# S5 mixer and ConvFFN layer: the SSM's output products with channels in partitions, and the GLU's operands split in place

## The chip, the cores and the metric

The kernel runs on one core of a Trainium2 chip. The metric is the device time of one execution in microseconds (us); lower is better. Engines are named as in the profile: PE is TensorE (PEld its weight loads), DVE is VectorE, ACT is ScalarE, POOL is GpSimd, SP is SyncE, which here only issues transfers.

## The reference, cut to what matters

One layer on a sequence of 2048 frames of 1024 channels with 16 meta tokens ahead of it: an S5 state-space mixer with a GLU, then a gated ConvFFN, both with a pre-RMSNorm and a residual.

```python
def s5_mixer(xn, w_in, lam_re, lam_im, log_dt, b_re, b_im, c_re, c_im, d_skip, w_glu):
    u = (xn @ w_in).reshape(bsz, L, S5_GROUPS, S5_GROUP)      # 64 groups of 16 channels
    ...                                                       # discretised a, b per group, 64 complex states
    _, _, s_re, s_im = lax.associative_scan(_complex_lin_combine, (a_re, a_im, bu_re, bu_im), axis=1)
    y = (einsum('ghp,blgp->blgh', c_re, s_re) - einsum('ghp,blgp->blgh', c_im, s_im) + d_skip * u)
    y = jax.nn.gelu(y.reshape(bsz, L, D_MODEL))
    a, g = jnp.split(y @ w_glu, 2, axis=-1)
    return a * jax.nn.sigmoid(g)

h = concatenate([meta, x])
h = h + s5_mixer(rms_norm(h, norm_mix), ...)
h = h + conv_ffn(rms_norm(h, norm_ffn), ...)                   # up, causal conv of 3, silu gate, down
return h[:, N_META:]
```

## The kernel before

**The sequence in chunks.** The 2048 frames are 128 chunks (index k) of 16 frames (index t). A "tile" is one frame position t of all 128 chunks: 128 frames by 1024 channels. The 1024 channels are eight blocks (`cb`), each of eight groups (`g`) of 16 channels (`h`). Fp32 values that enter fp16 products are split in a high and a low fp16 half, and three products (`mm3`, or the three pairs in `glu_mm`) stand for one.

**SSM, block by block** (loop over `p`, the block whose scan runs in that step). TensorE forms u of later blocks (`emit_u`), the chunk inputs of the next block (`emit_v`) and the output products of the block before (`emit_y(p - 1)`). DVE generates the matrices of the block (`gen_b`, `gen_c`) and runs the scan over chunks (`scan`). `emit_k` forms the convolution kernel inside a chunk, which goes to DRAM (`kd`) and comes back as a Toeplitz tile `tp` (`load_toep`: 8 transfers); `emit_z` moves the scanned states across partitions into `z` (4 transfers). All these transfers are issued by SP in program order.

**Output products** (`emit_y`). For each group: two products with the Toeplitz tile against `u`, of both halves of a chunk (f = 0, 1), and one with `ca` against `z`. The chunk index k is in the output's partitions, and 256 columns hold (t, h). All are fp32; each shows as two records per product in the profile. Two groups share one PSUM tile `yp`; ACT applies the GELU into `yf`. POOL issues one transfer per block to DRAM, `yd[t, k, channel]`: runs of 128 channels, 512 B. Ahead of the groups, `mp` forms the two meta tokens' y in the same way with channels in partitions.

**GLU, tile by tile** (`load_y`, `prep_y`, `glu_mm`, `glu_post`). `load_y` reads one tile's y (k in partitions, up to 4 KB per row). `prep_y` splits it in two fp16 halves `yh` (first half on ACT or, for the early parts, on DVE; second half on DVE), and SP issues two DMA transposes that write them with channels in partitions into `yT`, a tile with two buffers. `glu_mm` multiplies by the weights `wg` (two halves of `w_glu`, split by `split_wg`, either ACT with POOL or DVE alone): 96 products of 512 columns per tile, into four PSUM banks. Even tiles use the tags u and v, odd ones t and y, so tile t + 2 uses the banks of tile t. `glu_post` evicts them (ACT's sigmoid, DVE's product and residual), norms the tile and hands it on to the ConvFFN with more DMA transposes.

The early parts of tiles 0 and 1 run inside the last SSM steps: blocks 0 to 4 of tile 0 are split in the step of block 6, the rest up to block 6 at the end. The order of the later tiles is written out by hand:

```python
for t in range(1, T):
    ...
        prep_y(t + 2, gp_tile)
        ...
    if t == 4:
        glu_meta2(*ms)
    if t == 3:
        ms = glu_meta()
    ...
    glu_post(t)
    if t + 1 < T:
        glu_mm(t + 1)
```

`glu_meta` is the GLU of the two meta tokens: it splits their y into `ym`, 256 small products `gm` against `wg`, then sigmoid and residual. `glu_meta2` is their norm: DVE sets a tile `one` to ones, TensorE sums over partitions with it (`prm`).

**ConvFFN** (not touched): up products, convolution, down products in two passes over the sequence.

Lines of before used below: L113 `load_y`, L123, L125, L126, L128 `prep_y`, L137 `glu_mm`, L452 `transp`, L537 `scan`, L575 to L593 `emit_y`, L921, L922 `glu_post`, L979, L980, L984 `glu_meta`, L1007, L1009 `glu_meta2`.

Of the kernel before, what the change touches and what calls it, by code (L numbers as in the profile page):

```python
# [10 lines left out]
F16 = mybir.dt.float16  # L11
# [33 lines left out]
def tile_kernel(ctx: ExitStack, tc: tile.TileContext, x, meta, norm_mix, norm_ffn, w_in, lam_re, lam_im, log_dt,  # L45
# [15 lines left out]

    yd = dram.tile([T, P, D], F32, name="yd")
    ymd = dram.tile([P, 2, NCB], F32, name="ymd")
# [27 lines left out]
    def split_wg(i, pool, tag, bufs):  # L91

        dk, hh = divmod(i, 2)
        cs_ = slice(D * hh, D * hh + D)
        st = pool.tile([P, D], F32, tag=tag, bufs=bufs, name=f"gst{dk}_{hh}")
        PO.dma_start(out=st, in_=w_glu[0, dk * P:(dk + 1) * P, cs_])
        yield
        if wg_eng[0] is V:
            V.tensor_scalar(wg[0][:, dk, cs_], st, GS, None, op0=ALU.mult)
            V.scalar_tensor_tensor(wg[1][:, dk, cs_], st, GS, wg[0][:, dk, cs_], op0=ALU.mult, op1=ALU.subtract)  # L100
        else:
            A.activation(st, st, AF.Copy, scale=GS)
            A.copy(wg[0][:, dk, cs_], st)
            PO.tensor_tensor(wg[1][:, dk, cs_], st, wg[0][:, dk, cs_], op=ALU.subtract)
# [5 lines left out]

    def load_y(t, tile_of, d0=0, d1=DK):
        yts[t] = tile_of("yt", [P, D], F32, f"yt{t}_{d0}")
        SY.dma_start(out=yts[t][:, 0:P * (d1 - d0)], in_=yd[tile_of_step(t), :, P * d0:P * d1])  # L113

    def prep_y(t, tile_of, d0=0, d1=DK, eng=A):

        w = P * (d1 - d0)
        if t not in yT:
            yT[t] = gl.tile([P, 2, DK, P], F16, tag="yT", bufs=2, name=f"yT_{t}")
        yt = yts.pop(t)  # L120
        yh = [tile_of("yh", [P, D], F16, f"yh{t}_{d0}_{i}") for i in range(2)]
        if eng is A:
            A.activation(yh[0][:, 0:w], yt[:, 0:w], AF.Copy, scale=YS)  # L123
        else:
            V.tensor_scalar(yh[0][:, 0:w], yt[:, 0:w], YS, None, op0=ALU.mult)  # L125
        V.scalar_tensor_tensor(yh[1][:, 0:w], yt[:, 0:w], YS, yh[0][:, 0:w], op0=ALU.mult, op1=ALU.subtract)  # L126
        for i in range(2):
            SY.dma_start_transpose(out=yT[t][:, i, d0:d1], in_=yh[i][:, 0:w])  # L128

# [11 lines left out]
    with ExitStack() as c2:  # L141
# [424 lines left out]
        def emit_y(cb, mid=None):  # L566
# [12 lines left out]
            A.dma_start(out=ymd[:, :, cb], in_=mf)  # L579
            yf = s5.tile([P, T, G, T], F32, tag="yf", name=f"yf{cb}")  # L580
            for gp in range(4):
                yp = psum.tile([P, 2, 256], F32, tag="y", name=f"yp{cb}_{gp}")
                for i in range(2):
                    g = 2 * gp + i
                    PE.matmul(out=yp[:, i], lhsT=u[:, 1, g, 1:P + 1], rhs=tp[:, g], start=True, stop=False)
                    PE.matmul(out=yp[:, i, P:256], lhsT=u[:, 0, g, 1:P + 1], rhs=tp[:, g, 0:P], start=False, stop=False)
                    PE.matmul(out=yp[:, i], lhsT=z[:, g], rhs=ca[:, g, 1:T + 1].rearrange("p a b -> p (a b)"),
                              start=False, stop=True)
                A.activation(yf[:, :, 2 * gp:2 * gp + 2].rearrange("p t g h -> p g t h"),
                             yp.rearrange("p g (t h) -> p g t h", h=T), AF.Gelu_apprx_tanh)  # L590
                if mid:
                    mid(gp)
            PO.dma_start(out=yd[0:T, :, cb * P:(cb + 1) * P].rearrange("t k c -> k t c"),  # L593
                         in_=yf.rearrange("p t g h -> p t (g h)"))

# [97 lines left out]
        def s5_tile(kind, shape, dt, nm):  # L693
            if kind == "yt" and nm == "yt0_0":
                return ld.tile(shape, dt, tag="wst", bufs=1, name=nm)
            tag, bufs = ("us", 2) if kind == "yh" else ("U", 2) if nm[2] == "1" else ("S", 2)
            return s5.tile(shape, dt, tag=tag, bufs=bufs, name=nm)
# [12 lines left out]
        for p in range(NCB - 1):  # L710
# [22 lines left out]
            if pen:  # L733
                fills.append(prep_y(0, s5_tile, 0, NY[0], V) for _ in range(1))
            fills = itertools.chain(*fills)
# [37 lines left out]
        glu_mm(0, 3, NY[0])  # L773
        prep_y(1, s5_tile, 0, NY[1], V)
        prep_y(0, s5_tile, NY[0], NY[1], V)
        wg_split(12, 16, V)

# [121 lines left out]
    with ExitStack() as c3:  # L899
# [68 lines left out]
        def meta_load():  # L968
            for b in range(2):
                for tt in range(2):  # L970
                    SY.dma_start(out=ytm[64 * b:64 * b + 64, tt],
                                 in_=ymd.rearrange("(i t h) b cb -> b t i h cb", t=2, h=16)[b, tt])
            SY.dma_start(out=xm, in_=meta[14:16].rearrange("t (c p) -> (t c) p", p=P))
# [55 lines left out]
        for t in range(2):  # L1029
            prep_y(t, gp_tile, NY[1], DK)  # L1030
        load_y(2, gp_tile)
        for t in range(2):
            glu_mm(t, NY[1], DK)
        prep_y(2, gp_tile)
        load_y(3, gp_tile)
        meta_load()
        glu_post(0)
        for t in range(1, T):
            if t + 1 < T:
                load_x2(t + 1)  # L1040
            if t + 2 < T:
                prep_y(t + 2, gp_tile)
                if t + 3 < T:
# [329 lines left out]
```

## Time and profile before

| what | value |
|---|---|
| three timed runs | 2143.22, 2127.36, 2143.39 us; median 2143.22 |
| the profiled execution's own time | 2128.21 us |
| its span, first to last instruction | 2126.4 us |
| granted TensorE clock, mean | 0.962 |
| PE busy | 1925.9 us (91%) |
| DVE busy | 1518.7 us (71%) |
| ACT busy | 644.8 us (30%) |
| POOL busy | 689.3 us (32%) |

The stages of the span: norm, u and parameters up to about 150 us; the SSM steps up to about 437; the GLU up to 771, of which the part with full tiles begins at 437; the ConvFFN from 771 to the end. A row of the timeline gives start, duration, engine, line, operation, output and inputs, shape, count, and in brackets the idle time before it with what ended it. Matmul durations overlap: how long one takes is read from the starts. A row that begins with `SPq` is SP's transfer queue.

### The profile page before, as it was taken

The numbers are of one execution on the slowest core, as the hardware profiler recorded it, in microseconds if no ns is written. First come the engines' busy times: TensorE is split into PE (matmuls) and PEld (weight loads), VectorE is DVE, ScalarE is ACT, GpSimd is POOL, SyncE is SP. The second block draws the span as 40 slices with busy tenths as digits, with TensorE's granted clock in tenths as the row PEclk, the third lists the DMA queues.
The fourth block names the chain that finished last, engine by engine and source line by source line (L and its number), as shares of the span: only waits on it lengthen the run. The fifth ranks groups of instructions, "written<-read, shape, count | busy, mean of one in ns | idle before, by whom it ended". The sixth has DMA issues, their size and how long they took to land. (4 is left out here: it accounts for less than half of the span.)

```text
span 2126.4 us, 29078 instructions
## 1 busy us (share of the span) xinstructions
PE 1925.9 (91%) x10860; PEld 954.7 (45%) x10860; DVE 1518.7 (71%) x2084; ACT 644.8 (30%) x1083; POOL 689.3 (32%) x727
## 2 busy tenths in 40 slices
PE   4688999699999999999999867676999999999999
PEld 3456556455444444444444323232444444444444
DVE  4489988944443459999999987954466666668882
ACT  4432322312222234444344422212122223232110
POOL 5221211410000025554666774734100001116740
PEclk9998999799999999999999989888999999999999
DMA  9956666957665565444434659554733333336443
GB/s 203 196 116 132 146 127 150 224 155 171 132 157 134 137 166 181 158 147 152 149 127 151 170 156 267 156 168 150 232 104 101 103 100 104 101 103 159 133 121 98
DMA packets 333449, 315.50 MB, mean 148 GB/s; under 512 B 149740, under 2 KB 237372, under 8 KB 333308
## 3 DMA queue, kind: packets, MB, share of 16 engines
q1 hardware_dynamic: 315388, 271.59, 49.4%
q0 software_dynamic: 8496, 27.30, 4.7%
q10 hardware_dynamic: 9424, 14.76, 2.6%
q8 instruction: 85, 1.39, 0.3%
q14 instruction: 56, 0.46, 0.1%
HBM read 175.17 MB, written 102.69 MB: 131 GB/s over the span
## 5 line engine op out<-in xcount | busy, mean ns | idle before, releaser
L78 PE MATMUL p<-hc,wc 128*128 128x512 f16 x1232 | 468.8, 381 | 6.5 <-DVE wc L886 6.5
L76 PE MATMUL p<-hc,wc 128*128 128x512 f16 x1232 | 468.8, 381 | 1.9 <-DMA hc<-hl 1.9
L77 PE MATMUL p<-hc,wc 128*128 128x512 f16 x1232 | 468.6, 380 | 0.9 <-DMA hc<-hl 0.9
L137 PE MATMUL g<-wg,yT 128*128 128x512 f16 x1536 | 334.2, 380 | 0.8 <-DMA yT<-yh 0.8
L77 PE MATMUL po<-wc,act 128*128 128x512 f16 x616 | 244.7, 397 | 80.4 <-DVE wc L886 80.4
L76 PE MATMUL po<-wc,act 128*128 128x512 f16 x616 | 243.5, 395 | 8.5 <-DVE res L1323 3.7
L78 PE MATMUL po<-wc,act 128*128 128x512 f16 x616 | 244.4, 397 | 0.0
L137 PEld LDWEIGHTS <-yT 128*128 128x128 f16 x1536 | 150.5, 98 | 182.9 <-issue 2.6
L886 DVE SCALAR_TENSOR_TENSOR wc<-fst,wc 128x512 f16<-128x512 f32 x209 | 199.0, 966 | 44.4 <-ACT wc L880 34.5
L880 ACT ACTIVATE wc<-fst 128x512 f16<-128x512 f32 x209 | 125.6, 625 | 245.0 <-POOL fst L847 120.3
L78 PEld LDWEIGHTS <-wc 128*128 128x128 f16 x1232 | 120.8, 98 | 154.7 <-DVE wc L886 8.8
L77 PEld LDWEIGHTS <-wc 128*128 128x128 f16 x1232 | 120.7, 98 | 139.9 <-issue 1.9
L76 PEld LDWEIGHTS <-wc 128*128 128x128 f16 x1232 | 120.6, 98 | 140.1 <-issue 3.5
L76 PE MATMUL u<-hnT,win 128*128 128x512 f16 (+2 forms) x352 | 113.1, 331 | 26.9 <-DMA hnT<-hl 17.0
L78 PEld LDWEIGHTS <-act 128*128 128x128 f16 x616 | 62.3, 101 | 163.5 <-issue 98.4
L1218 DVE TENSOR_TENSOR hc<-hc,hc 128x512 f32<-128x512 f32 x66 | 86.5, 1323 | 68.7 <-POOL hc L1216 42.7
L1219 ACT CAST act<-hc 128x512 f16<-128x512 f32 x88 | 54.2, 618 | 244.9 <-DVE hc L1218 148.0
L77 PE MATMUL u<-hnT,win 128*128 128x512 f16 (+2 forms) x352 | 112.9, 331 | 9.9 <-DMA hnT<-hl 9.9
L78 PE MATMUL u<-hnT,win 128*128 128x512 f16 (+2 forms) x352 | 112.7, 330 | 0.0
L1095 ACT ACTIVATE act<-hu,cwt 128x1024 f32<-128x1024 f32 x44 | 54.6, 1241 | 178.5 <-DVE hu L1187 129.8
L1095 ACT ACTIVATE y<-hu,cwt 128x1024 f32<-128x1024 f32 x44 | 54.6, 1241 | 162.3 <-DVE hu L1187 122.8
L1216 POOL TENSOR_TENSOR hc<-act 128x512 f32<-128x512 f16 x66 | 90.5, 1378 | 37.7 <-DVE hc L1218 37.7
(366 smaller groups left out, 3024.7 us busy)
## 6 DMA issues: line engine op xcount, KB each, us to landing
wcd<-wc SPq DMA_DIRECT2D x231, 256.0 KB, 2.3
wc<-wcd SPq DMA_DIRECT2D x231, 256.0 KB, 2.6
fst<-in_ffn_w_down_dram SPq DMA_DIRECT2D x49, 512.0 KB, 4.7
fst<-in_ffn_w_up_dram SPq DMA_DIRECT2D x44, 512.0 KB, 5.0
ud<-us SPq DMA_DIRECT2D x32, 258.0 KB, 4.8
U<-ud SPq DMA_DIRECT2D x16, 516.0 KB, 6.9
Toep<-kd SPq DMA_DIRECT2D x64, 128.0 KB, 5.5
yd<-yf POOLq DMA_DIRECT2D x8, 1024.0 KB, 6.5
```

The costliest lines, as they stand in the source:

```text
L76: PE.matmul(out=ps, lhsT=sh, rhs=mh, start=first, stop=False)
L77: PE.matmul(out=ps, lhsT=sh, rhs=ml, start=False, stop=False)
L78: PE.matmul(out=ps, lhsT=sl, rhs=mh, start=False, stop=last)
L137: PE.matmul(out=gps[t][o], lhsT=yT[t][:, a, dk], rhs=wg[b][:, dk, 512 * o:512 * o + 512], start=(dk == 0 and a + b == 0), stop=(dk == DK - ...
L880: A.activation(w[:, 0], src, AF.Copy, scale=GS)
L886: V.scalar_tensor_tensor(w[:, 1], src, GS, w[:, 0], op0=ALU.mult, op1=ALU.subtract)
L1095: A.activation(y, hu[:, 2:18], AF.Identity, bias=cwt[:, 3, c:c + 1], scale=cwt[:, 2, c:c + 1])
L1216: PO.tensor_tensor(t_, act16[:, fa_, ra, 1], act16[:, fb, rb, 1], op=op)
L1218: V.tensor_tensor(s_, s_, t_, op=ALU.add)
L1219: A.copy(act16[:, fd, rd, 0], s_)
```

## The change

The output products swap their operands: the Toeplitz tile and `ca` become the weights, `u` and `z` (columns: the 128 chunks) stream through. The output then has (frame of a half chunk, h) in its 128 partitions, chunks k in its columns, and a tile per half chunk `r`: five products of 128 columns per group in place of three of 256, 128 and 256. `yd` is laid out as block, half, partition, group, chunk, so that a block is written in runs of 4 KB, and a frame's 128 channels of a block come back as 128 partitions of 512 B, with the channels in the order (h, g). `load_y` therefore lands with channels in partitions, `prep_y` writes both halves straight into `yT`, and its DMA transposes and the tile `yh` are gone. `w_glu`'s rows and the meta tokens' y are loaded in the order (h, g) too.

```diff
-    yd = dram.tile([T, P, D], F32, name="yd")
+    yd = dram.tile([NCB, 2, P, G, P], F32, name="yd")
...
-        PO.dma_start(out=st, in_=w_glu[0, dk * P:(dk + 1) * P, cs_])
+        PO.dma_start(out=st, in_=w_glu[0, dk * P:(dk + 1) * P, cs_].rearrange("(g h) n -> h g n", h=16))
...
     def load_y(t, tile_of, d0=0, d1=DK):
         yts[t] = tile_of("yt", [P, D], F32, f"yt{t}_{d0}")
-        SY.dma_start(out=yts[t][:, 0:P * (d1 - d0)], in_=yd[tile_of_step(t), :, P * d0:P * d1])
+        r, t8 = divmod(tile_of_step(t), 8)
+        SY.dma_start(out=yts[t][:, 0:P * (d1 - d0)].rearrange("p (b k) -> p b k", k=P),
+                     in_=yd[d0:d1, r, 16 * t8:16 * t8 + 16].rearrange("b h g k -> (h g) b k"))

-    def prep_y(t, tile_of, d0=0, d1=DK, eng=A):
+    def prep_y(t, d0=0, d1=DK, eng=A):
...
-        yh = [tile_of("yh", [P, D], F16, f"yh{t}_{d0}_{i}") for i in range(2)]
+        hi, lo = (yT[t][:, i, d0:d1].rearrange("p b k -> p (b k)") for i in range(2))
         if eng is A:
-            A.activation(yh[0][:, 0:w], yt[:, 0:w], AF.Copy, scale=YS)
+            A.activation(hi, yt[:, 0:w], AF.Copy, scale=YS)
         else:
-            V.tensor_scalar(yh[0][:, 0:w], yt[:, 0:w], YS, None, op0=ALU.mult)
-        V.scalar_tensor_tensor(yh[1][:, 0:w], yt[:, 0:w], YS, yh[0][:, 0:w], op0=ALU.mult, op1=ALU.subtract)
-        for i in range(2):
-            SY.dma_start_transpose(out=yT[t][:, i, d0:d1], in_=yh[i][:, 0:w])
+            V.tensor_scalar(hi, yt[:, 0:w], YS, None, op0=ALU.mult)
+        V.scalar_tensor_tensor(lo, yt[:, 0:w], YS, hi, op0=ALU.mult, op1=ALU.subtract)
...
-            yf = s5.tile([P, T, G, T], F32, tag="yf", name=f"yf{cb}")
+            yf = s5.tile([P, 2, G, P], F32, tag="yf", name=f"yf{cb}")
             for gp in range(4):
-                yp = psum.tile([P, 2, 256], F32, tag="y", name=f"yp{cb}_{gp}")
+                yp = psum.tile([P, 2, 2, P], F32, tag="y", name=f"yp{cb}_{gp}")
                 for i in range(2):
                     g = 2 * gp + i
-                    PE.matmul(out=yp[:, i], lhsT=u[:, 1, g, 1:P + 1], rhs=tp[:, g], start=True, stop=False)
-                    PE.matmul(out=yp[:, i, P:256], lhsT=u[:, 0, g, 1:P + 1], rhs=tp[:, g, 0:P], start=False, stop=False)
-                    PE.matmul(out=yp[:, i], lhsT=z[:, g], rhs=ca[:, g, 1:T + 1].rearrange("p a b -> p (a b)"),
-                              start=False, stop=True)
-                A.activation(yf[:, :, 2 * gp:2 * gp + 2].rearrange("p t g h -> p g t h"),
-                             yp.rearrange("p g (t h) -> p g t h", h=T), AF.Gelu_apprx_tanh)
+                    for r in range(2):
+                        for f in range(r + 1):
+                            PE.matmul(out=yp[:, r, i], lhsT=tp[:, g, P * (r - f):P * (r - f) + P],
+                                      rhs=u[:, 1 - f, g, 1:P + 1], start=f == 0, stop=False)
+                        PE.matmul(out=yp[:, r, i], lhsT=ca[:, g, 8 * r + 1:8 * r + 9].rearrange("p a b -> p (a b)"),
+                                  rhs=z[:, g], start=False, stop=True)
+                A.activation(yf[:, :, 2 * gp:2 * gp + 2], yp, AF.Gelu_apprx_tanh)
...
-            PO.dma_start(out=yd[0:T, :, cb * P:(cb + 1) * P].rearrange("t k c -> k t c"),
-                         in_=yf.rearrange("p t g h -> p t (g h)"))
+            PO.dma_start(out=yd[cb].rearrange("r p g k -> p r g k"), in_=yf)
```

Three places show how the instructions stand. First TensorE's order at block 7's first group (`U` and `Toep` are u and the Toeplitz tile, `CA` and `Z` the other pair; the two DMA queues are those of z). Before:

```order
L585 MATMUL yp_0_4334<-Toep_4113,U_3848 128x256 [waits Activation_49]
L586 MATMUL yp_0_4334<-Toep_4113,U_3848 128x128
L587 MATMUL yp_0_4334<-CA_4065,Z_4266 128x256 [waits DMAHW6_49,DMAHW0_49]
L585 MATMUL yp_0_4334<-Toep_4113,U_3848 128x256
L586 MATMUL yp_0_4334<-Toep_4113,U_3848 128x128
L587 MATMUL yp_0_4334<-CA_4065,Z_4266 128x256 [waits DMAHW7_49,DMAHW2_49]
```

After:

```order
L588 MATMUL yp_0_4442<-U_3944,Toep_4205 128x128 [waits Activation_49]
L590 MATMUL yp_0_4442<-Z_4374,CA_4157 128x128 [waits DMAHW6_49,DMAHW4_49]
L588 MATMUL yp_0_4442<-U_3944,Toep_4205 128x128 x2
L590 MATMUL yp_0_4442<-Z_4374,CA_4157 128x128
L588 MATMUL yp_0_4442<-U_3944,Toep_4205 128x128
L590 MATMUL yp_0_4442<-Z_4374,CA_4157 128x128 [waits DMAHW5_49,DMAHW0_49]
```

The wait for z now stands behind one product of 128 columns instead of two with 384.

Second, ACT's order from the first half of tile 2 to the norm of tile 0 (`yt` is the loaded y, `sg` the sigmoid's output, `g` the PSUM banks). Before:

```order
L123 ACTIVATE yh_0_0_4589<-yt_0_4562 128x1024 [waits DMAHW7_49,DMAHW5_49,DVE_49]
L921 ACT_TABLE_LOAD
L921 ACTIVATE sg_4602<-g_2_4076 128x512 [waits PE_49]
L921 ACTIVATE sg_4602<-g_3_4077 128x512 [waits PE_49]
L925 ACTIVATE sg_4602,ss_0_4603<-x_0_4434 128x1024 [waits DMASW2_49,DVE_49]
```

After:

```order
L126 ACTIVATE yT_4696<-yt_0_4670 128x1024 [waits DMAHW5_49,DVE_49,PE_49]
L922 ACT_TABLE_LOAD
L922 ACTIVATE sg_4704<-g_2_4168 128x512
L922 ACTIVATE sg_4704<-g_3_4169 128x512
L926 ACTIVATE sg_4704,ss_0_4705<-x_0_4550 128x1024 [waits DMASW2_49,DVE_49]
```

No row changes its place; the wait for PE has moved from the sigmoids to the first half, which stands ahead of them and of the table load.

Third, DVE's order around the meta tokens (`ym` their halves, `one` the tile of ones). Before, around tiles 5 and 6:

```order
L126 SCALAR_TENSOR_TENSOR yh_0_1_4905<-yt_0_4776,yh_0_0_4904 128x1024 [waits DMAHW7_49,DMAHW6_49,Activation_49]
L980 SCALAR_TENSOR_TENSOR ym<-ytm,ym 128x8x2 [waits DMAHW5_49,Activation_49]
L994 TENSOR_TENSOR gss<-gms 128x32 [waits Activation_49]
...
L126 SCALAR_TENSOR_TENSOR yh_0_1_5321<-yt_0_4910,yh_0_0_5320 128x1024 [waits DMAHW7_49,DMAHW6_49,Activation_49]
L1007 MEMSET one 128x128
L1011 TENSOR_SCALAR rm<-prm 128x2 [waits PE_49]
```

After:

```order
L129 SCALAR_TENSOR_TENSOR yT_4997<-yt_0_4870,yT_4997 128x1024 [waits DMAHW5_49,Activation_49]
L979 SCALAR_TENSOR_TENSOR ym<-ytm,ym 128x8x2 [waits DMAHW0_49,Activation_49]
L993 TENSOR_TENSOR gss<-gms 128x32 [waits Activation_49]
...
L129 SCALAR_TENSOR_TENSOR yT_5409<-yt_0_5000,yT_5409 128x1024 [waits DMAHW3_49,Activation_49]
L1006 MEMSET one 128x128
L1010 TENSOR_SCALAR rm<-prm 128x2 [waits PE_49]
```

Here too the order is the same; the second half, which waits for ACT's first half of the same tile, stands ahead of `ym` and of `one`, and ACT's first half waits for PE as at the second place.

More of the change, by code (lines that the diff above doesn't have):

```diff
@@ L693, in s5_tile @@
         def s5_tile(kind, shape, dt, nm):
-            if kind == "yt" and nm == "yt0_0":
+            if nm == "yt0_0":
                 return ld.tile(shape, dt, tag="wst", bufs=1, name=nm)
-            tag, bufs = ("us", 2) if kind == "yh" else ("U", 2) if nm[2] == "1" else ("S", 2)
+            tag, bufs = ("U", 2) if nm[2] == "1" else ("S", 2)
             return s5.tile(shape, dt, tag=tag, bufs=bufs, name=nm)
@@ L733, in tile_kernel @@
             if pen:
-                fills.append(prep_y(0, s5_tile, 0, NY[0], V) for _ in range(1))
+                fills.append(prep_y(0, 0, NY[0], V) for _ in range(1))
             fills = itertools.chain(*fills)
@@ L773, in tile_kernel @@
         glu_mm(0, 3, NY[0])
-        prep_y(1, s5_tile, 0, NY[1], V)
-        prep_y(0, s5_tile, NY[0], NY[1], V)
+        prep_y(1, 0, NY[1], V)
+        prep_y(0, NY[0], NY[1], V)
         wg_split(12, 16, V)
@@ L968, in meta_load @@
         def meta_load():
[L969 to L972, printed above, removed]
+            for tt in range(2):
+                SY.dma_start(out=ytm[:, tt], in_=ymd.rearrange("(i t h) b c -> t h b i c", t=2, h=16)[tt])
             SY.dma_start(out=xm, in_=meta[14:16].rearrange("t (c p) -> (t c) p", p=P))
@@ L1029, in tile_kernel @@
         for t in range(2):
-            prep_y(t, gp_tile, NY[1], DK)
+            prep_y(t, NY[1], DK)
         load_y(2, gp_tile)
@@ L1033, in tile_kernel @@
             glu_mm(t, NY[1], DK)
-        prep_y(2, gp_tile)
+        prep_y(2)
         load_y(3, gp_tile)
@@ L1041, in tile_kernel @@
             if t + 2 < T:
-                prep_y(t + 2, gp_tile)
+                prep_y(t + 2)
                 if t + 3 < T:
```

## Prediction

> **What bounds the kernel now.** I read the windows by stage first, then TensorE's timeline in the two stages that the change touches, then the other engines at the places where it hands over to them.
>
> Three stages (columns: length; then busy microseconds and instructions of PE, weight load, DVE, ACT, POOL; granted clock, DMA share, GB/s):
> ```profile
> 150.00:361.00 211.00, 188.13 (x1546) 124.39 (x1546) 193.23 (x426) 57.05 (x119) 34.87 (x60) 0.95 0.68 137
> 361.00:437.00 76.00, 54.22 (x424) 42.14 (x425) 69.74 (x114) 27.59 (x41) 27.30 (x23) 0.80 0.91 216
> 437.00:757.00 320.00, 318.95 (x1697) 147.95 (x1695) 133.93 (x166) 76.12 (x111) 23.13 (x49) 0.99 0.62 144
> ```
> The SSM steps (150 to 361) are held by VectorE and TensorE in turn. The last two steps (361 to 437) are VectorE's: busy 69.74 of 76. The GLU (437 to 757) is TensorE's alone: busy 318.95 of 320, with VectorE at 42%. The removed transposes lie nearly all in that third stage, so what they can give back there is bounded by its 1.05 us of idle. The transposes, the one wait of TensorE for them in this stage, and the transfer queue's longest wait on its side:
> ```profile
> L128 SPq DMA_TRANSPOSE yT<-yh x38: 1096/1303/2742, 373.5 to 730.7; - x38
> ...
> 471.25 9.02 PE L137 MATMUL g<-wg,yT 128*128 128x512 f16 x41 [0.75 <-DMA yT<-yh]
> ...
> SPq L128 <- PE g L137: 62.9, 12, 11.0
> ```
> 0.75 us is all that TensorE waited for a transposed y here. The third row says the reverse: 12 times, 62.9 us in all, the transpose was waiting for TensorE, that is, for a free yT buffer. Whoever writes yT inherits that wait.
>
> **What goes.** 38 transposes leave SP's queue and the transfer engines. The first run at 373.5, where VectorE sets the end with its scans of blocks 6 and 7; in the GLU TensorE does. I count their removal as zero; the cover is VectorE's 69.74 of 76 and TensorE's 318.95 of 320. What is late next, where the 0.75 us stood, is worked out under A.
>
> **The output products.** Per group, one 256-, one 128- and one 256-column fp32 product become five of 128: 640 columns both ways.
> ```profile
> 435.58 0.59 PE L585 MATMUL yp<-Toep,U 128*128 128x256 f32 x2
> 436.01 0.38 PE L586 MATMUL yp<-Toep,U 128*128 128x128 f32 x2
> 436.23 0.60 PE L587 MATMUL yp<-CA,Z 128*128 128x256 f32 x2
> 436.67 13.54 PE L137 MATMUL g<-wg,yT 128*128 128x512 f16 x62
> ...
> 118.78 1.04 PE L452 MATMUL wt<-ident,wit 128*128 128x128 f32 x8
> ```
> By starts, 256 columns take 0.43 us and 128 take 0.22, so five take 1.09 against 1.09 for the three now. The last row is eight 128-column fp32 records, each with weights of its own: seven intervals in 0.77 us, 0.110 each, against 0.11 for half of L586. So I take **0**; the weight loads hide.
>
> On the other side, the first group now reaches its z product after one product, not two of 384 columns: 0.43 us that ran while z was awaited comes behind that wait. Block 7's wait:
> ```profile
> 422.42 0.38 PE L586 MATMUL yp<-Toep,U 128*128 128x128 f32 x2
> 426.85 0.70 PE L587 MATMUL yp<-CA,Z 128*128 128x256 f32 x2 [4.05 <-DMA Z<-S]
> ```
> From there TensorE runs into the GLU, so **+0.43** in full. Earlier blocks waited too, four times in the middle steps, for the 2.8 us in this row:
> ```profile
> PE yp L587 <- DMA Z<-S: 2.8, 4, 1.3
> ```
> Where VectorE is the bound this is hidden; blocks 3 and 4 feed a TensorE-bound stretch, and their shift reaches VectorE's scan 6 once: **+0.5** (0 to 0.9).
>
> **The y blocks.** Writes now go in 4 KB runs instead of 512 B, reads in 512 B runs instead of up to 4 KB. Only one read is on VectorE's chain:
> ```profile
> 368.86 0.49 DVE L125 TENSOR_SCALAR yh<-yt 128x640 f16<-128x640 f32 x1 [0.95 <-DMA yt<-yd]
> ...
> U<-ud SPq DMA_DIRECT2D x16, 516.0 KB, 6.9
> ...
> x<-in_x_dram POOLq DMA_DIRECT2D x16, 512.0 KB, 4.2
> ```
> Rows of 516 B against rows of 4 KB: 2.7 us more for 512 KB, so up to 1.7 for the 320 KB; at the lower end 0. U's median includes its own queueing, so I take the middle, **+0.9**. VectorE waits there already, so this passes on to scan 7 and to z of block 7.
>
> **yT written by ACT and DVE.** The halves now go straight into yT, which has two buffers: for tile t+2, ACT's first half must wait until the products of tile t are done, and it stands ahead of tile t's sigmoids in ACT's queue. In the steady state that costs nothing: TensorE has tile t+1 to do, 96 products at 0.216 = 20.7 us, while ACT's and DVE's chain grows by 1.0 and 1.2. It costs where something that TensorE needs next is queued behind the halves. There are three such places.
>
> *A, tile 2.* Only 12 products (2.6 us) stand between the end of tile 0 and tile 2, which needs tile 0's PSUM banks.
> ```profile
> 460.11 1.06 ACT L123 ACTIVATE yh<-yt 128x1024 f16<-128x1024 f32 x1 [6.26 <-DMA yt<-yd]
> 461.18 1.28 ACT L921 ACT_TABLE_LOAD   x1
> ...
> 467.73 1.09 ACT L921 ACTIVATE sg<-g 128x512 f32<-128x512 f32 x2 [5.27 <-PE g L137]
> ...
> 468.36 0.69 DVE L922 SCALAR_TENSOR_TENSOR sg<-g,sg 128x512 f32<-128x512 f32 x1 [5.94 <-ACT sg L921]
> ...
> 469.70 0.68 DVE L922 SCALAR_TENSOR_TENSOR sg<-g,sg 128x512 f32<-128x512 f32 x1
> ```
> Now half and table load were over long before 467.73. After, both follow it: half to 468.7, table load to 470.0, sigmoids from 470.0. DVE releases the first bank 0.63 + 0.69 later, 471.3, and the second at 470.0 + 1.97 + 0.68 = 472.65. TensorE starts at 471.3, as now, but its second product waits until 472.65 instead of 471.47: **+1.2**.
>
> *B, the meta tokens' GLU behind tile 3.*
> ```profile
> 507.57 1.06 ACT L123 ACTIVATE yh<-yt 128x1024 f16<-128x1024 f32 x1 [7.00 <-DMA yt<-yd]
> 508.53 0.20 ACT L979 ACTIVATE ym<-ytm 128x16 f16<-128x16 f32 x1
> ...
> 508.66 1.23 DVE L126 SCALAR_TENSOR_TENSOR yh<-yt,yh 128x1024 f16<-128x1024 f32 x1 [6.83 <-ACT yh L123]
> 509.80 0.17 DVE L980 SCALAR_TENSOR_TENSOR ym<-ytm,ym 128x16 f16<-128x16 f32 x1
> ...
> 512.70 0.34 PE L984 MATMUL gm<-ym,wg 128*128 128x4 f16 x8
> ...
> 542.48 17.82 PE L137 MATMUL g<-wg,yT 128*128 128x512 f16 x81
> ...
> 563.41 1.08 ACT L921 ACTIVATE sg<-g 128x512 f32<-128x512 f32 x2 [10.35 <-PE g L137]
> ```
> ym is ready 2.7 us early now. After, ACT's half starts when tile 3 ends: a sigmoid so released comes 0.2 us after TensorE's next product (542.48 + 96 x 0.216 = 563.2, against 563.41), so at 512.9; ym's second half follows 2.23 + 0.17 later, 515.3. TensorE stands from 512.7 to about 515.35: **+2.65** (1.8, if ACT were released four products early, to 4).
>
> *C, the meta tokens' norm behind tile 4.* DVE's memset of the ones, which TensorE's small product needs, stands behind the second half of tile 6:
> ```profile
> 534.44 1.05 ACT L123 ACTIVATE yh<-yt 128x1024 f16<-128x1024 f32 x1
> ...
> 536.90 0.17 DVE L1007 MEMSET one<- 128x128 f32 x1
> ...
> 542.34 0.28 PE L1009 MATMUL prm<-sm,one 128*128 128x2 f32 x2
> ```
> Start of the half to the end of the memset: 2.63. From 542.54 that gives 545.2 instead of 542.34: **+2.9**. Here TensorE then resumes dense products, and after a gap its clock may halve:
> ```profile
> 361.71 0.43 PE L575 MATMUL mp<-U,Toep 128*32 128x1 f32 x32 [2.92 <-DMA Z<-S]
> ...
> 364.28 1.06 PE L585 MATMUL yp<-Toep,U 128*128 128x256 f32 x2
> ...
> 366.33 0.59 PE L585 MATMUL yp<-Toep,U 128*128 128x256 f32 x2
> ...
> 512.00:520.00 8.00, 7.72 (x262) 7.21 (x259) 0.00 (x0) 0.06 (x1) 0.00 (x0) 0.78 0.88 161
> ```
> After 2.92 us of idle, products ran at half rate for some 3 us, a loss of 1.5. The gap at C is as long: **+1.5** (0 to 1.7). At B it costs nothing more: the meta products run at half clock already (0.78).
>
> The Trainium skill, "TensorE: Matmul & The Clock Gate" (Part 1, The HAM clock gate), says the clock halves after at least one idle window of about 3.4 us. By that rule neither gap would halve it, and the sum would be 1.5 lower. The row at 361.71 halves after 2.92 (with 0.27 more behind it), so I go by the row.
>
> **Sum.** 0.43 + 0.5 + 0.9 + 1.2 + 2.65 + 2.9 + 1.5 = **+10.1 us**. The profiled execution took 2128.21 (span 2126.4), so 2138.3 by its own measure. The three timed runs have two groups, 2127.36 and 2143.22/2143.39; the profile belongs to the lower, the median to the upper. The feed-forward stages behind are untouched, so I expect both groups to persist and take the median's: 2143.2 + 10.1 = **2153**.
>
> **Rivals.**
> *The gaps cancel against a shorter head.* Against the +10, relief on the transfer engines (91% busy from 361 to 437) could bring Toeplitz and z blocks sooner; TensorE waited for those in the steps from 150 to 361, beside the 2.8 above:
> ```profile
> PE mp L575 <- DMA Toep<-kd: 12.9, 3, 7.1
> ```
> If half of these 15.7 us went, +10.1 becomes +2.2: 2145. Against it: no transpose of y runs before 373.5, and only the written runs' size differs earlier.
> *Faster.* VectorE's instructions near POOL's subtractions are stretched in the last two steps:
> ```profile
> 372.62 2.73 DVE L537 TENSOR_TENSOR S<-S,sta6k 128x112 f32<-128x112 f32 x1
> ...
> 378.88 0.33 DVE L537 TENSOR_TENSOR S<-S,sta6k 128x96 f32<-128x96 f32 x1
> ```
> About 2.4 us each, and POOL makes eight such subtractions. If earlier transfers moved all of these to idle moments of VectorE: -19, sum -9, 2134. VectorE has next to no idle moments there, so unlikely.
> *Slower: weight loads show.* The 2 x 2 added records per group could each expose a weight load of 0.14 us.
> ```profile
> L452 PEld LDWEIGHTS wt<-ident,wit x96: 137/140/143, 187.2 to 377.3; 128*128 128x128 f32 x96
> ```
> 32 per block x 0.14 = 4.5 us; on the path in blocks 3, 4 and 7 and partly in the others, about 4 blocks: +18, in all +28, 2171. It decides if records of 128 columns come more than 0.11 us apart; L452's eight at 0.110 speak against it. The Trainium skill, "TensorE: Matmul & The Clock Gate" (Part 3, The mechanism), speaks for this rival: weight loads overlap running products only when their row groups differ; L452's row, with one row group throughout, does not agree.
> *The change doesn't do what it says* is excluded: no transpose of y is left in SP's order.
>
> **How the numbers follow.** Chances: forecast 0.64, cancelling 0.18, slower by exposed loads 0.08, faster 0.06, the rest (a gap longer than worked out, tile after tile) 0.04. Lowest: the lower group with B at 1.8, C without the clock, A, the reads and the head at nothing and 5 us of relief, 2126. Highest within 8 in 10: the upper group with every upper bound, +19, 2162. About 1% (21 us) is what a measurement tells from no change. Faster by over 1% needs the third case and more: 0.05. Slower: the exposed loads and the rest, 0.12. Same: 0.83.
>
> **What would show it.** In the GLU stage three new gaps on TensorE: 1.2 more at tile 2, 2.6 before the meta products, 2.9 before the norm's product, with the half rate behind it; the releasers ACT and DVE, not a transfer. The first half of yT beginning about 0.2 us after each tile ends. In the products, 0.22 us per 128 columns. Wrong would be: those gaps absent, the GLU stage not 8 us longer, products spaced over 0.11, or block 7's z arriving at another time than some 1 us later.

## The result, and the profile after

The changed kernel takes **2147.9 us** (median of 9 runs, 2144.22 to 2156.28) against 2133.7 for the kernel before in 9 runs beside it: ratio 1.0062 (95% interval 1.0038 to 1.0085), that is +13 us (8 to 18). A later set of runs gave 1.0080 (1.0057 to 1.0103), +17 (12 to 22). The difference is real and by both ratios below 1%: same, on the slow side, as the prediction had it. The forecast time of 2153 us, range 2126 to 2162, holds the measured one; its sum of +10.1 lies low in the first interval and below the second.

The profiled execution took 2149.12 us (span 2147.3). The last two of the prediction's three windows (same columns; the first 8 us of the second now still belong to block 7):

```profile
361.00:437.00 76.00, 48.79 (x454) 40.67 (x453) 68.62 (x112) 26.26 (x38) 26.45 (x24) 0.76 0.97 199
437.00:757.00 320.00, 312.82 (x1677) 148.65 (x1677) 126.86 (x159) 72.53 (x106) 21.57 (x47) 0.97 0.47 116
```

The DMA share of the GLU window fell from 0.62 to 0.47: the transposes are gone. TensorE, busy 318.95 of 320 there before, is now busy 312.82. Its timeline shows where it stands idle, from the first product behind block 7 to the first product of the ConvFFN:

```profile
444.93 33.83 PE L138 MATMUL g<-wg,yT 128*128 128x512 f16 x156
479.95 0.38 PE L138 MATMUL g<-wg,yT 128*128 128x512 f16 x1 [1.19 <-DVE sg L923]
481.28 41.38 PE L138 MATMUL g<-wg,yT 128*128 128x512 f16 x191 [0.95 <-DVE sg L923]
525.15 0.34 PE L983 MATMUL gm<-ym,wg 128*128 128x4 f16 x8 [2.49 <-DVE ym L979]
...
532.16 23.34 PE L138 MATMUL g<-wg,yT 128*128 128x512 f16 x96
558.05 0.59 PE L1008 MATMUL prm<-sm,one 128*128 128x2 f32 x2 [2.55 <-DVE one L1006]
558.50 231.01 PE L138 MATMUL g<-wg,yT 128*128 128x512 f16 x1056
789.35 0.38 PE L76 MATMUL p<-hc,wc 128*128 128x512 f16 x1
```

The three gaps are at the places A, B and C of the prediction, and the releaser is each time what was named there: DVE behind ACT's late sigmoids, `ym`, `one`. How the wait passes on shows at C, in the timelines of ACT and DVE:

```profile
555.54 1.06 ACT L126 ACTIVATE yT<-yt 128x1024 f16<-128x1024 f32 x1 [8.90 <-PE g L138]
...
556.63 1.23 DVE L129 SCALAR_TENSOR_TENSOR yT<-yt,yT 128x1024 f16<-128x1024 f32 x1 [8.73 <-ACT yT L126]
557.83 0.17 DVE L1006 MEMSET one<- 128x128 f32 x1
```

ACT's first half waits for TensorE's last product of tile 4 (over at 555.50), DVE's second half for ACT, the memset behind it for DVE, and TensorE for the memset. The stretch from 444.93 to 789.35 is 344.4 us long. Before, the same stretch ran from 436.67 (quoted above) to

```profile
770.57 0.38 PE L76 MATMUL p<-hc,wc 128*128 128x512 f16 x1
```

333.9 us. So the GLU costs **+10.5**: A 2.14 in place of 0.75, +1.4; B +2.5; C +2.55 and 0.3 for the norm's product at half rate; 2.75 in the 1056 products behind it (231.01, against 228.25 with no gap, in the runs below); 0.9 in the 96 between, which took anything from 22.4 to 23.6 in the profiles of this document, so that this 0.9 can't be put down to the change.

The start of the GLU also came 8.3 us later, and the first profiles differ by 20.9 us in span, more than the medians do. TensorE's timeline in a second profile of before, taken in the experiments, tells why this must not be read as the change:

```profile
438.91 1.22 PE L587 MATMUL yp<-CA,Z 128*128 128x256 f32 x2 [7.86 <-DMA Z<-S]
450.00 20.24 PE L137 MATMUL g<-wg,yT 128*128 128x512 f16 x93
```

The same kernel started its GLU at 450.00 there, not 436.67 (time 2145.66, not 2128.21), and ended it 334.05 us later. **The GLU's length repeats within 0.2 us in before's two profiles; what lies ahead of it, called the head from here on, differs by 13 us between them.** What happens in the GLU can be read from one profile each, to within 1 or 2 us. What happens in the head must be judged by many runs, or by durations inside it. The ConvFFN, which is not touched, differs as well: from its first product to the end of the span 1355.8 and 1359.9 us in before's two profiles, 1358.0 in the changed kernel's. Where a cost of the head is worked out below as the total less the GLU, some 4 us of it can be the ConvFFN's.

### The profile page after: what moved, and what is told of

Same layout as the page of the kernel before. It is cut to its first block, busy times and chain, and to the rows that moved or that the text cites. A ratio compares the mean times of both kernels' runs of the same rounds, so it can differ in the third digit from the quotient of the medians.

```text
span 2147.3 us, 29499 instructions
## 1 busy us (share of the span) xinstructions
PE 1937.2 (90%) x11116; PEld 971.8 (45%) x11116; DVE 1519.8 (71%) x2084; ACT 644.1 (30%) x1083; POOL 686.0 (32%) x727
## 5 line engine op out<-in xcount | busy, mean ns | idle before, releaser
L129 DVE SCALAR_TENSOR_TENSOR yT<-yt,yT 128x1024 f16<-128x1024 f32 (+4 forms) x19 | 20.1, 1056 | 124.1 <-ACT yT L126 123.9
```

The source lines that it names most:

```text
L129: V.scalar_tensor_tensor(lo, yt[:, 0:w], YS, hi, op0=ALU.mult, op1=ALU.subtract)
```

## The experiments

In all of them the GLU's length is counted as above. "Before" in a ratio is the kernel before, run beside the experiment.

**1. A third yT buffer.**

```diff
-yT[t] = gl.tile([P, 2, DK, P], F16, tag="yT", bufs=2, ...)
+pool, bufs = (gp, 1) if t % 3 == 2 else (gl, 2)
+yT[t] = pool.tile([P, 2, DK, P], F16, tag="yT", bufs=bufs, ...)
```

> The changed kernel with a third yT buffer, so that the halves of tile t + 2 need not wait for the products of tile t. Theory (the three gaps of the GLU, with the half rate behind them, are the inherited wait): all three gaps go, and the GLU, from the first product after block 7 to the first product of the ConvFFN, takes about 334 us, as before the change (333.9), in place of 344.4; the total falls by 10.5, from 2147.9 to about 2137.5, and what stays of the difference to 2133.7 lies ahead of the GLU. Rival (the gaps come from y's loads in short rows, which also land late): the releasers become transfers, the gaps stay at over half their length, and the total falls by under 5, to over 2143. Second rival (the half rate comes from power or from the longer dense stretch, not from the gaps): gaps go, 6 us, but the products behind tile 4 stay at 231 us for 1056 in place of 228.

Measured: 2132.94, ratio to before 1.0009 (0.9982 to 1.0037). TensorE's timeline:

```profile
442.32 75.27 PE L139 MATMUL g<-wg,yT 128*128 128x512 f16 x348
...
524.27 23.12 PE L139 MATMUL g<-wg,yT 128*128 128x512 f16 x96
547.24 0.28 PE L1009 MATMUL prm<-sm,one 128*128 128x2 f32 x2
547.38 228.25 PE L139 MATMUL g<-wg,yT 128*128 128x512 f16 x1056
775.47 0.38 PE L76 MATMUL p<-hc,wc 128*128 128x512 f16 x1
```

All gaps are gone, and the half rate behind C with them. The GLU takes 333.15, 11.3 less than in the changed kernel and 0.75 less than before: about the one wait for a transposed y, which is what the removal gives there. That the wait for a free buffer makes the gaps is shown, and the total bears it out, 1.0009 in place of 1.0062. Both rivals fall, with one remnant: the 96 products behind the meta products take 23.12 with no gap at all (22.45 in before's first profile, 22.81 in its second), so the 0.9 there is not the gap's.

**2. Two buffers, but `ym` and `one` issued ahead of the halves of tile 5.**

```diff
+if t == 3:
+    ym, one = meta_split(), meta_one()    # ym's two halves; the memset, in a buffer of its own
 if t + 2 < T:
     prep_y(t + 2)
```

> The changed kernel, two buffers as they were, but the split of the meta tokens' y and the memset of the ones are issued ahead of the halves of tile 5 (the ones get a buffer of their own). Theory (a gap arises only where a thing that TensorE needs next is queued behind the halves): gaps B and C go with the half rate behind them, gap A at tile 2 stays at 2.1; the GLU takes 344.4 - 2.5 - 0.9 - 2.85 - 2.9 = 335.3, the total falls by 9, to about 2139. Rival (two buffers are too few in themselves: a gap at each tile or one at the next tile replaces these): the GLU falls by under 4 us, to over 340, with TensorE waiting for yT. Third possibility (the loss behind the meta products is their own, since 96 products behind them took 22.45 before also): 0.9 of the 9 stays.

Measured: 2140.82, ratio 1.0066 (1.0045 to 1.0087); GLU 337.7.

```profile
548.22 0.28 PE L1013 MATMUL prm<-sm,one 128*128 128x2 f32 x2
548.36 0.38 PE L138 MATMUL g<-wg,yT 128*128 128x512 f16 x1
550.85 227.87 PE L138 MATMUL g<-wg,yT 128*128 128x512 f16 x1055 [2.12 <-DVE rm L1015]
```

B and C go, A stays (1.19 and 0.95 again), as the theory said. But a new gap of 2.12 stands one product behind C: `rm`, which frees the PSUM bank that tile 5's second product takes, is itself queued behind the half of tile 6. In the changed kernel the gap at C covered it. So the GLU gave 6.7 of the 9, and the theory's own rule (what TensorE needs next is queued behind a half) names the rest; I had not listed every such instruction. The total does not show the gain: against the runs of before beside each, 1.0066 here and 1.0062 and 1.0080 for the changed kernel. The 6.7 rest on the trace alone. The half rate did not follow this gap: 1055 products in 227.87 are at full rate.

**3. y in long rows.**

```diff
-yd = dram.tile([NCB, 2, P, G, P], F32, name="yd")
+yd = dram.tile([2, P, G, NCB, P], F32, name="yd")
```

> The changed kernel with yd laid out as half, partition, group, block, chunk: y is then read in rows of 2.5 to 4 KB and written in runs of 512 B, the products and the halves being as changed. Theory (the read of 512 B rows holds VectorE in the last SSM steps): VectorE's wait for tile 0's first five blocks falls from 4.0 to about 1 us, block 7's z lands some 2 us earlier after its issue, and the GLU starts 3 to 5 us earlier: total 2143 to 2145. Rival (VectorE's wait comes from the products of blocks 3 and 4 being later, and z's from the queue): the wait stays over 3 us, and the total at 2147.9 within 2. The GLU stays at about 344 by both.

Measured: 2147.49, ratio 1.0087 (1.0066 to 1.0107), no gain; GLU 344.4. VectorE's timeline at the first read of tile 0's y, in the changed kernel:

```profile
374.17 2.45 DVE L128 TENSOR_SCALAR yT<-yt 128x640 f16<-128x640 f32 x1 [4.02 <-DMA yt<-yd]
```

In this one:

```profile
373.11 0.49 DVE L128 TENSOR_SCALAR yT<-yt 128x640 f16<-128x640 f32 x1 [3.58 <-DMA yt<-yd]
```

In the run with three buffers, which reads rows of 512 B as the changed kernel does:

```profile
368.87 0.49 DVE L129 TENSOR_SCALAR yT<-yt 128x640 f16<-128x640 f32 x1 [0.96 <-DMA yt<-yd]
```

Long rows leave 3.58; short rows can have 0.96, the wait of before's first profile. Rows of 512 B are not what holds it. The 0.96 is the exception, though: the five other profiles of the changed layout with short rows show 2.76 to 4.26 at this place, the seven of before's layout 0 to 2.21. So the wait did grow with the change; by what, no run shows. It need not cost much: the two forms under 6 have it at 3.93 and 4.26 and take no longer than before.

**4. The kernel before with five products.** Output orientation, y's layout and transposes are those of before; each group's products are cut and ordered as in the change.

```diff
-PE.matmul(out=yp[:, i], lhsT=u[:, 1, g, 1:P + 1], rhs=tp[:, g], ...)               # 256 columns
-PE.matmul(out=yp[:, i, P:256], lhsT=u[:, 0, g, 1:P + 1], rhs=tp[:, g, 0:P], ...)   # 128
-PE.matmul(out=yp[:, i], lhsT=z[:, g], rhs=ca[:, g, 1:T + 1]..., ...)               # 256
+for r in range(2):                                                                 # 128 each
+    for f in range(r + 1):
+        PE.matmul(out=yp[:, i, P * r:P * r + P], lhsT=u[:, 1 - f, g, 1:P + 1], rhs=tp[:, g, P * (r - f):P * (r - f) + P], ...)
+    PE.matmul(out=yp[:, i, P * r:P * r + P], lhsT=z[:, g], rhs=ca[:, g, 8 * r + 1:8 * r + 9]..., ...)
```

> The kernel before, with its output products cut into five of 128 columns per group, in the changed kernel's order of steps (the z product comes after one product, the second half after it), and nothing else changed: chunks stay in partitions, y's layout, the transposes and the halves are those of before. Theory (ahead of the GLU the change costs through its products: the z product is reached sooner, and records of 128 columns run at 1.117 us per group in place of 1.083): the output products of blocks 3 and 4 take 2 to 2.5 us longer than the 10.9 and 9.4 of before, the GLU starts 3 to 5 us later; total 2133.7 + 4 = about 2138. Rival (y's layout in DRAM costs it): blocks 3 and 4 stay within 0.7 of before, total 2133.7 within 2. Third possibility (the spacing of 1.117 comes from weights that change with each record; here the weights are u and z, two or three in turn): the wait shows but the spacing stays at 1.083, and half of the 4 us.

Measured: 2144.18, ratio **1.0078** (1.0056 to 1.0100): +16.6, four times what was expected, with nothing else of the change in it. The spacing is that of the changed kernel, 1.116 per group, so the third possibility falls; blocks 3 and 4 took 13.6 and 10.7 us in its profile, 12.3 and 10.8 in the second one below, in place of 11.4 and 9.9 in before's first (counted as in the table under 6). In its profile TensorE also waited 9.5 us for a transposed y, so a second profile was taken, along with one of before:

> The kernel before with five products per group, again, for a second profile. In the first one TensorE waited 9.5 us for transposes of tile 1 at the start of the GLU, where before waited 0.75. Theory (with a later head the transposes come on the path, so that taking them away is worth that much): the wait is there again, over 5 us. Rival (an accident of that execution, the slowest of six): under 2 us, and a total under 2143.

> The kernel before, unchanged, for a second profile of its head. Theory (the change costs some 4 to 8 us ahead of the GLU): the GLU's first product behind block 7 starts at 436 to 438 again, and z of block 7 lands within 5 us of its issue (4.3 in the first profile; 6 to 8 in the five profiles with five products per group). Rival (the first profile caught a short head, and the head varies by itself): the GLU starts at 439 to 443, and z takes 6 us or more.

The second profile's execution took 2144.71, and in TensorE's timeline

```profile
484.67 41.61 PE L137 MATMUL g<-wg,yT 128*128 128x512 f16 x192 [0.78 <-DMA yT<-yh]
```

is its only wait for transposes; its GLU is 333.9 long. The 9.5 did not come again (the total of 2143 asked for was missed by 1.7), and with a GLU as long as before's the loss lies in the head. Before's second profile went to the rival, as told above: the head varies by itself, and its start of the GLU at 450.00 lies even beyond the rival's 443.

**5. Which part of the five products costs: z early, or more records?** In each PSUM tile of two groups, all products with u go first and those with z last, for the kernel before and for its form with five products:

```diff
 for i in range(2):           # two groups of a PSUM tile
     ...                      # the products with the Toeplitz tile
-    ...                      # the product(s) with z
+for i in range(2):
+    ...                      # the product(s) with z
```

> The kernel before, three products per group, with the two products with z of each PSUM tile behind the four with u. Theory (in the head TensorE pays for z being reached early): z is reached 0.65 us later in each block, TensorE's waits for it shrink, block 7 ends 0.65 earlier: total 1 to 3 below before. Rival (the head is set by VectorE's scans and by the landing of z of block 7, which varied from 4.3 to 12.8 us after its issue in the two profiles of before): no difference that five rounds show, and the same two groups of times, 2124 to 2134 and 2136 to 2146.

> The kernel before with five products of 128 columns per group as before (that run: 2144.2 against 2128.6), now with all products with u of a PSUM tile ahead of those with z. Theory A (the 15 us came from reaching z after one product): the loss falls to under 4 us. Theory B (it came from the number of records, which make each block 1 to 2 us longer, so that block 6 ends late and its write of y runs beside z of block 7): the loss stays at 10 us or more, nearly all runs in the upper group of before's times.

Measured: three products with z last 2127.24, ratio **0.9956** (0.9941 to 0.9972); five with z last 2131.8, ratio 0.9988 (0.9963 to 1.0014). Theory A holds: the 16.6 us are gone with the order alone, the number of records unchanged; B falls. With three products the gain is 9 us by the ratio, where the theory had 1 to 3: its direction is right, its size is not explained. The fastest of the six runs (2124.80) is no faster than the fastest of before (2124.42); what is missing are before's slower runs, since none of the six is over 2130.3. Block 4's products, first in TensorE's timeline of the changed kernel (first profile):

```profile
321.57 0.49 PE L590 MATMUL yp<-Z,CA 128*128 128x128 f32 x2 [1.03 <-DMA Z<-S]
...
323.82 1.06 PE L588 MATMUL yp<-U,Toep 128*128 128x128 f32 x4
...
326.87 0.61 PE L588 MATMUL yp<-U,Toep 128*128 128x128 f32 x4
```

Then in that of the kernel with five products and z last:

```profile
320.50 1.60 PE L588 MATMUL yp<-Toep,U 128*128 128x128 f32 x12
321.94 1.06 PE L594 MATMUL yp<-CA,Z 128*128 128x128 f32 x8
322.83 1.50 PE L588 MATMUL yp<-Toep,U 128*128 128x128 f32 x12
325.06 1.50 PE L588 MATMUL yp<-Toep,U 128*128 128x128 f32 x12
```

In the first TensorE has one product to do before it must stop for z, and in this profile goes on at half rate (four records 1.06, against 0.61 later). In the second the wait is covered. The records themselves cost little: two groups take 2.23 us from 322.83 to 325.06, 1.115 per group, against 1.09 for three products; 0.25 per block.

**6. The changed kernel with three buffers and z later.** Where two products share weights they become one (the first half of the Toeplitz tile over both halves of u): four products per group, z reached after 384 columns; then also z last.

```diff
-for r in range(2):
-    for f in range(r + 1):
-        PE.matmul(out=yp[:, r, i], lhsT=tp[:, g, P * (r - f):P * (r - f) + P], rhs=u[:, 1 - f, g, 1:P + 1], ...)
+PE.matmul(out=yp[:, :, i], lhsT=tp[:, g, 0:P], rhs=u[:, :, g, 1:P + 1], ...)
+PE.matmul(out=yp[:, 0, i], lhsT=tp[:, g, P:2 * P], rhs=u[:, 1, g, 1:P + 1], ...)
```

> The changed kernel with the third yT buffer, and its output products merged where they have the same weights: the first half of the Toeplitz tile goes once over both halves of u (256 columns), so a group has four products of 256, 128, 128 and 128 columns, and reaches z after 384 columns, as before the change. To this end the half chunks stand in reverse order in the output tile and in yd. Theory (ahead of the GLU the change costs through five products: 1.117 us per group in place of 1.083, and z reached after 128 columns): the products of a block take 1 to 1.5 us less than in the run with three buffers (12.6, 11.9, 10.2, 12.8 for blocks 2 to 5), the GLU starts some 3 us earlier than its 442.3, total about 2130 against its 2133. Rival (the head is held by the transfers of z and of the weights, not by products): block times fall but the GLU starts at 441 to 443, and the total stays at 2133.

> As the run with shared weights, and in each PSUM tile of two groups all products with u first, the four with z last, so that z is reached after 768 columns (1.3 us) in place of 384 (0.65). Theory (z's wait costs TensorE): another 0.65 us less wait in each of blocks 1 to 4, and 0.65 at block 7, which passes into the GLU in full; total 1 to 2 below the run with shared weights, about 2128.5, as before the change or just under it. Rival (VectorE and the transfers hold the head): no difference between the two runs that five rounds show.

Measured: 2130.47, ratio 0.9991 (0.9973 to 1.0008), and 2129.76, ratio 0.9983 (0.9961 to 1.0004). The totals move as the theory says, but by less than five rounds separate from before or from each other. In the first the GLU starts at 440.95, 1.4 us ahead of the 442.32 with five products, where 3 were expected; blocks 2 to 4 are 0.4 to 2.0 us shorter and block 5 is 2.1 longer. The sums over blocks speak more plainly. The time of the output products of blocks 0 to 5, each from the start of its first meta product to the end of its last product as the timeline gives it (start and duration of the last row), waits included:

| z reached after | kernel | six blocks, us | time, ratio to before |
|---|---|---|---|
| 128 columns | changed, two profiles | 79.0, 75.1 | 1.0062, 1.0080 |
| 128 | changed, third buffer | 75.8 | 1.0009 |
| 128 | changed, new queue order | 77.4 | 1.0066 |
| 128 | changed, y in long rows | 78.2 | 1.0087 |
| 128 | before, five products, two profiles | 79.1, 77.8 | 1.0078 |
| 384 | before, two profiles | 69.6, 71.6 | 1 |
| 384 | before, late write (under 7) | 70.3 | 1.0018 |
| 384 | changed, third buffer, shared weights | 70.4 | 0.9991 |
| 768 | the same, z last | 67.9 | 0.9983 |
| 768 | before, z last | 65.3 | 0.9956 |
| 768 | before, five products, z last | 66.5 | 0.9988 |

Three levels, 75 to 79, 70 to 72 and 65 to 68, whatever the layout of y and the number of products. The totals do not follow them alone: with the third buffer 75.8 goes with a time like before's, and in the changed layout z last shows no gain in time.

**7. The write of block 6's y behind z of block 7** (in before; SP issues it, not POOL), to explain before's two groups of times.

```diff
-PO.dma_start(out=yd[0:T, :, cb * P:(cb + 1) * P]..., in_=yf...)
+write = ...                  # the same transfer, returned by emit_y for block 6
 emit_z(p)
+write(SY)
```

> The kernel before, with the write of block 6's y issued by SP right behind the four transfers of block 7's z, not by POOL as soon as block 6 is done. Theory (before's two groups of times, 2124 to 2134 and 2136 to 2146, are the cases in which that write, 1 MB in runs of 512 B, is over when z of block 7 is issued or runs beside it: in the fast profile it was issued 4.6 us ahead of z and z landed after 4.3 us, in the slow one 0.8 ahead and z landed after 12.8): the upper group goes, all runs 2122 to 2134. Rival (the groups come from something else): a third of the runs stay above 2136. Against both: tile 1's y now lands later; if that holds up the GLU, TensorE waits for yT by more than the 0.7 us of before.

Measured: 2138.75 (2134.37 to 2144.33), ratio 1.0018 (1.0000 to 1.0036). z of block 7 landed 3.9 us after its issue (419.74 to 423.68), but the late write cost elsewhere, as TensorE's timeline shows:

```profile
431.57 0.70 PE L585 MATMUL yp<-Toep,U 128*128 128x256 f32 x2 [1.58 <-ACT yf L589]
...
444.46 25.82 PE L137 MATMUL g<-wg,yT 128*128 128x512 f16 x111 [3.09 <-DMA yT<-yh]
```

No run is left in the lower of before's groups, and 8 of 12 lie in the upper, so the theory's 2122 to 2134 fails; but the late write brought the wait of 3.09 for yT that was to count against both, so it does not decide for the rival. And in the changed kernel z of block 7 took 6.9 us though that write had been issued 9 us ahead. What makes before's two groups stays open.

**8. The changed kernel again.**

> The changed kernel again, beside new runs of before, to settle its difference in time and with it what its head costs. The GLU's 10.5 us are seen in the trace; if the total differs from before by 10.5 to 13, the change's head costs up to 3 us, as the run with three buffers (+1.9, interval -4 to +8, its GLU 0.7 shorter than before's) has it; by 14 or more, the head costs 4 and more. The three gaps again at 1.2 and 1.0, 2.5 and 2.55 us.

Measured: 2152.63, ratio 1.0080 (1.0057 to 1.0103). The gaps are 1.19, 0.95, 2.49 and 2.55 again; the GLU is 342.9 long, since the products behind C lost only 1.1 (229.39). By this set the head costs 8, by the first 3, by the run with three buffers 2.6 (1.9, and 0.7 that its GLU is shorter). Each of these differences has an interval of 5 to 6 us to either side, so they do not contradict one another.

## Why the prediction held, point by point

**The GLU** carried it. A: +1.2 predicted, +1.4 measured. B: +2.65, +2.5. C: +2.9, +2.55 as a gap, and 0.3 in the norm's product at half rate. Half rate behind C: 1.5 (0 to 1.7) predicted; 2.75, 2.75 and 1.1 in three profiles, above the range in two. The mechanism, a wait inherited with the buffer that the transposes had borne, is shown by experiments 1 and 2. For B I said that no half rate would be added; the 0.9 seen there also comes without a gap, so that stands. The reason I gave does not: 0.78 was a mean. The meta products begin at a granted clock of 1.00, which falls to 0.50 some 3.7 us into them in before and 1.8 us in the changed kernel's first profile.

**The head** was the weak part: +1.83 predicted, 3 to 8 measured. The step that failed is the +0.43 and +0.5 for z after one product. I counted the 0.43 of shifted work once per block, and only for blocks 3, 4 and 7. Measured, six blocks take 4 to 10 us longer than with z after 384 columns, 7 by the means; shift and pace (0.43 + 0.25 per block) explain 4.1 of it. The rest I had not priced; half rate behind the wait for z is part of it in some blocks, and no run takes it apart. In before's layout that order and the five records cost 16.6 in all, and nothing with z last. One of my signs of being wrong also came: block 7's z product started at 434.30 and 434.51 in the changed kernel's two profiles, some 7.5 us behind the 426.85 of before and not 1. It was no test, since before's own second profile has 438.91.

**The read in short rows**, +0.9: VectorE's wait there did grow, in five of six profiles with short rows by 1.8 to 3.3 us over the 0.95 of before, but the rows are not the reason, since long ones had 3.58.

**The products' pace at 0** was nearly right: 0.25 per block. The rival of exposed weight loads is out: 1.115 per group, where it needed 0.14 for each of the added records.

**The removed transposes at 0** were right in the GLU (0.75, as its one wait said). In the head not quite: with five products and z early, before's layout costs +16.6 and the changed layout with three buffers +1.9. Something in the rest of the change gives back 9 to 14 us there (16.6 less the head's 3 to 8); with z last it gives nothing (0.9988 and 0.9983). In the profiles the meta products of block 6 start 35 to 38 us behind those of block 5 in the changed layout, 44 and 47 in before's with five products, 42 and 46 in before itself, 36 and 38 in before's layout with five and three products and z last, 40 with the late write. TensorE waits at that place, and no run here takes the wait apart.

**The cancelling rival** (0.18) therefore has something for it, a shorter head that works against the loss, but not its +2.2; that relief of the transfer engines makes the head shorter is not shown. Its time of 2145 is nearer to the measured 2147.9 than my 2153, for the reason that follows. **The base** was wrong: I added 10.1 to 2143.2, the upper of what I took for two groups. More runs show a lower and an upper heap with hardly a gap (of 23 in the last set, 15 from 2124 to 2136, 7 from 2138 to 2142, one at 2152); the median lies in the lower one, 2128.6 to 2133.9 in four sets, and the changed kernel's 15 runs, 2144 to 2161, show no second group. A base some 10 too high made up for a sum 3 to 7 too low: that the time came out within 5 us is luck, where the gaps of the GLU are not. The upper end of the range was wrong as well: the upper bounds that I gave add up to 12.8, not 19, so the range should have ended at 2156.

## What to carry to other kernels

Whoever writes a buffer in place of a transfer inherits the transfer's wait for it to be free, and with it holds up all that is queued behind on a compute engine: list every such instruction that another engine needs next, or add a buffer. In a sum of products put those whose operands arrive last at the end of the PSUM tile: that order was worth 0.44% here by itself in the kernel before, more than the layout, and the version with it and nothing else of the change has the lowest ratio of all that ran; in the changed layout with three buffers the step from 384 to 768 columns showed no difference in time. Before pricing a shift of one microsecond in a stage, see whether two executions of the same kernel agree there.

## What the runs showed of the hardware

The clock behind a gap, by windows (columns as in the prediction, the granted clock third from the end). In the changed kernel, in gap B, in gap C, and behind it:

```profile
522.66:525.15 2.49, 0.00 (x1) 0.00 (x0) 1.31 (x2) 1.16 (x2) 0.00 (x0) 1.00 0.00 0
555.50:557.50 2.00, 0.01 (x1) 0.00 (x0) 0.87 (x1) 1.06 (x1) 0.00 (x0) 1.00 0.92 229
557.50:558.05 0.55, 0.00 (x0) 0.00 (x0) 0.50 (x2) 0.00 (x0) 0.00 (x0) 0.63 1.00 300
558.00:562.00 4.00, 3.95 (x11) 1.73 (x12) 1.82 (x6) 1.19 (x3) 0.72 (x1) 0.50 0.05 15
562.00:566.00 4.00, 4.00 (x15) 1.52 (x14) 1.79 (x4) 1.15 (x2) 0.74 (x2) 0.69 0.33 131
```

In its second profile, behind gap C:

```profile
558.00:562.00 4.00, 3.39 (x10) 1.55 (x11) 1.86 (x7) 1.19 (x3) 0.72 (x1) 0.57 0.19 58
562.00:566.00 4.00, 4.00 (x21) 1.76 (x19) 2.07 (x4) 1.15 (x2) 0.46 (x2) 1.00 0.26 105
```

In the run with the new queue order, with its gap of 2.12 from 548.74:

```profile
548.30:555.00 6.70, 4.58 (x24) 2.06 (x23) 3.96 (x9) 2.25 (x4) 0.72 (x1) 1.00 0.39 104
```

The 0.63 ahead of the norm's product is a mean of 1.00 and 0.50: the clock halved inside gap C, some 2.1 us behind the last product (2.1 to 2.3 in the three profiles that have this gap), and the small product, which took 0.45 in place of 0.14, already ran at half rate. The half rate lasted 2.2 to 5.5 us behind it (a loss of 1.1 to 2.75). Yet a gap of 2.12 us with the new queue order left the clock at 1.00, and so did gap B with its 2.49; the length of a gap alone does not decide. In the head, a wait of 1.03 for z in block 4 was followed by half rate in one profile, where 0.76 and 0.94 in others were not. The Trainium skill, "TensorE: Matmul & The Clock Gate" (Part 1, The HAM clock gate), lets the clock fall after at least one idle window of about 3.4 us: at C 2.1 to 2.3 us were enough, and the measurement decides. It also calls the window free-running, so that the cost varies from run to run: with 2.75, 2.75 and 1.1 behind the same gap, the runs agree.
